# 512-column matmuls for both token halves in gate and up

## The chip, the cores and the metric

One core of a Trainium2 chip runs the whole kernel. The metric is device time in microseconds of one execution, the median of several. Engines are named as in the profile: PE (TensorE matmuls; PEld its weight loads), DVE (VectorE), ACT (ScalarE), POOL (GpSimd), SP (SyncE, which here only issues transfers). SBUF is the on-chip memory of 128 partitions, PSUM the matmuls' accumulator memory; a bank of it holds 512 fp32 columns.

## The reference

One decoder layer on 512 tokens of width 1024 in float32: a mixer (retention heads beside indexed sparse attention) with a residual LayerNorm, and then the feed-forward part, which the change is about:

```
gate, up = jnp.split(x @ w_gate_up, 2, axis=-1)        # x: 512 x 1024, w_gate_up: 1024 x 5632
ffn = (jax.nn.silu(gate) * up) @ w_down                # 2816 hidden features
return layer_norm(DEEPNORM_ALPHA * x + ffn, ln_ffn_gain, ln_ffn_bias)
```

## The kernel before

**fp32 by parts.** PE multiplies float32r operands, so each operand is split into a high part (ACT casts it) and a low part (the rest: DVE subtracts, or ACT writes minus the high part and a DMA issued by POOL adds the source onto it). A product is high x high + low x high + high x low, three matmuls for each block of 128 of the inner dimension. `split`, line 84, does this.

**Gate and up by seven products.** x and the weights are cut into 2 x 2 blocks: two halves of 256 tokens, two halves of 512 inner features, and the gate and the up column of a tile pair; the four outputs (gate and up of both token halves) come from seven products in place of eight (Strassen's scheme in Winograd's form). The stage goes over NF = 22 tiles of 128 hidden features, `order` gives their sequence, and `g_load(n)` brings a tile's gate and up weights (1 MB) into `graw[n]`, one of three buffers. The token side is made once in `parts`: "11", "12", "22" are blocks of x, "s1" to "s4" sums of them; each has a high and a low half, [partition, high or low, k, 256 tokens]. The weight side is made for each tile: B is gate's two blocks as they are, A, C and D come from the sums of `g_sum` (four DVE operations of 512 columns) and from up. `g_conv(n, kind)` splits them, two blocks of 512 columns each for A, B and C and one for D, into buffers of which each of the high and the low kind has four.

`g_mm(n, acc, kind, i, q, first)`, line 849, is one product: 12 matmuls of 256 columns, four k times (high, low) with the high tokens and high with the low tokens, into bank `acc`. A tile has banks a, b (PSUM tag "d", four banks in all) and c (tag "u", four banks). `g_cycle(n)`, line 883, issues one tile's products on PE, in this order in the steady state: A0(n) into a; A1(n) into c; B0(n+1) into a(n+1); C0(n) into a; B1(n+1) into b(n+1); C1(n) into a; D(n) into c. Between them a copy of bank a is taken three times, as the sums of the scheme need: after B0 (`g_t1`, to h1), after A0 (t2), after C0 (t7), and silu reads it at the end (h2). On DVE `g_add1` adds b to h1, t7 gets c, and `g_end(n-1)` adds c to t2 and multiplies: h1 = silu(gate) x up for one token half, h2 for the other. `hT(n)` is where h1 and h2 lie (`hu`).

The order of all engines is written out by hand (the schedule is manual: each engine takes its instructions in program order, and semaphores hold one back until its inputs are there and its buffer is free). Tiles n < FIRST = 4 go beside the end of the mixer and have special cases in `g_cycle`; 4 to 21 are the steady state. Behind the loop `prepare_down` splits the first blocks of w_down and of h, interleaved with the last tile by `next(between)`, and the down projection follows: matmuls of 512 columns for blocks m = 0 to 3 and 10 (`conv_w`, `conv_h`, `d_mm`), then a scheme of seven products for the rest.

SP issues the weight loads in program order; POOL issues the accumulating DMAs. In the steady state before, POOL has none, since all of `g_conv` there uses DVE.

Of the kernel before, what the change touches and what calls it, by code (L numbers as in the profile page):

```python
# [53 lines left out]
def hybrid_layer_kernel(ctx: ExitStack, tc: tile.TileContext, xT, x, pos, w0, wf, wt, wo,  # L54
# [761 lines left out]
    def g_sum(n, eng=V, which=slice(0, 4)):
        if n >= NF:
            return
        g, u = graw[n][:, 0], graw[n][:, 1]
        if n not in gsum:  # L820
            gsum[n] = [tmp(f"gs{n}_{i}") for i in range(4)]
        t = gsum[n]
        for dst, a, b in ((0, u[:, :S], g[:, :S]), (1, u[:, S:], t[0]), (2, u[:, S:], u[:, :S]), (3, g[:, S:], t[1]))[which]:
            eng.tensor_tensor(t[dst], a, b, op=ALU.subtract)  # L824
# [24 lines left out]
    def g_mm(n, acc, kind, i, q, first):
        h, l = gw[n, kind]  # L850
        steps = [(k, a, b) for k in range(4) for a, b in ((h, 0), (l, 0), (h, 1))]
        if n == 0:
            steps.sort(key=lambda x: x[2])
        for j, (k, a, b) in enumerate(steps):
            T.matmul(gp[n][acc], lhsT=a[:, i * S + k * P:i * S + k * P + P], rhs=parts[q][:, b, k],  # L855
                     start=first and j == 0, stop=j == 11, skip_group_check=True)

    def g_open(n):
        h = hT(n)
        gp[n] = {"a": psd(f"ga{n}")[:, :Q], "b": (psu if n < FIRST else psd)(f"gb{n}")[:, :Q], "h1": h[:, :Q], "h2": h[:, Q:]}  # L860

    def g_t1(n):
        A.copy(gp[n]["h1"], gp[n]["a"])

    def g_add1(n):
        h1 = gp[n]["h1"]
        V.tensor_tensor(h1, h1, gp[n]["b"], op=ALU.add)
# [8 lines left out]

    def g_end(n):
        g = gp[n]
        V.tensor_tensor(g["t2"], g["t2"], g["c"], op=ALU.add)
        V.tensor_tensor(g["h1"], g["h1"], g["t2"], op=ALU.mult)  # L880
        V.tensor_tensor(g["h2"], g["h2"], g["t7"], op=ALU.mult)

    def g_cycle(n, between=None):
# [10 lines left out]
        A.copy(gp[n]["t2"], gp[n]["a"])  # L894
# [16 lines left out]
        c = gp[n]["c"]  # L911
        if n == NF - 1:
            c = tmp("gc")[:, :Q]
            A.copy(c, gp[n]["c"])
            g_mm(n, "c", "D", 0, "s4", False)
        A.copy(gp[n]["t7"], gp[n]["a"])
# [8 lines left out]
        V.tensor_tensor(gp[n]["t7"], gp[n]["t7"], c, op=ALU.add)  # L925
# [60 lines left out]
    def combine(q, b, eng=V):  # L986
        if q in ("s2", "s3"):
            csum[q, b] = tmp(f"c{q}_{b}")
        src = {"s3": (kept["11", b - 2], "21"), "s2": ("22", csum.get(("s3", b))), "s1": (kept["11", b - 2], csum.get(("s2", b))),
               "s4": (kept["12", b - 2], csum.get(("s2", b)))}[q]  # L990
# [1 line left out]
        eng.tensor_tensor(csum[q, b], in0, in1, op=ALU.add if q == "s1" else ALU.subtract)
# [103 lines left out]
    def conv_w(c, k):  # L1096
        if k == 10 and c == 0:
            wprep((c, k), d10)
        else:
            t, i = (r5b, 2) if k == 10 else (draw[c, k // 2], 2 * (k % 2))  # L1100
            wprep((c, k), [t[:, i:i + 2].rearrange("p k c -> p (k c)")])

    def conv_h(m):
# [141 lines left out]
        V.scalar_tensor_tensor(y[b], in0=y[b], scalar=mv[:, 0:1], in1=gf[:, 0], op0=ALU.subtract, op1=ALU.mult)  # L1245

    def prepare_down():
        conv_w(0, 0)
        conv_h(0)
        yield  # L1250
        conv_w(0, 1)
        conv_h(1)
        yield
# [257 lines left out]
```

## Time and profile before

| what | value |
|---|---|
| median of 3 runs (lowest, highest) | 619.25 us (618.81, 619.79) |
| the profiled execution: own time, span | 619.74 us, 617.9 us |
| PE clock granted, mean | 0.996 |
| x's parts and tiles 0 to 3 (273 to 312.4 us of the span) | PE idle 0.64 us in all |
| tiles 4 to 21 (about 312 to 498 us) | PE without idle time |
| DMA share over ten of these tiles (332.6 to 433.3 us) | 0.30 |

The profile is one execution, on the hardware's profiler. A row of a timeline is start and duration in us, engine, line of the kernel, operation, tile written <- tiles read, shapes; in square brackets the idle time of the engine before it and what ended it. A row with xN holds N instructions in a row. In rows grouped by line the numbers at the end are busy time in us and the mean of one in ns, and then the idle time before them. A row of windows gives, for a stretch of the span, the busy us of each engine with its instruction count, the clock granted to PE, the mean busy share of the 16 DMA engines, and GB/s. A DMA row ends with the KB of one transfer and the median us from issue to landing. Rows of PE overlap, since the end of one matmul lies in the next; the distance of two starts is what a matmul costs in a stream.

### The profile page before, as it was taken

How to read it: one execution, taken by the hardware profiler on the slowest of the kernel's cores; microseconds unless marked ns; L12 is line 12 of the kernel's file. 1: busy time of each engine (PE TensorE's matmuls, PEld its weight loads, DVE VectorE, ACT ScalarE, POOL GpSimd, SP SyncE). 2: the span in 40 equal slices, each digit the busy share in tenths (PEclk: the TensorE clock that was granted, in tenths of full speed). 3: DMA queues.
4: the chain of work that ended last, by engine and by line, in shares of the span. 5: the costliest groups of instructions: out<-in, count | busy, mean ns of one | idle time of the engine just before them, and what ended most of it. 6: DMA issues, size and time to landing. Idle time of an engine off the chain costs nothing.

```text
span 617.9 us, 9846 instructions
## 1 busy us (share of the span) xinstructions
PE 608.2 (98%) x3732; PEld 545.6 (88%) x3732; DVE 512.8 (83%) x953; ACT 323.0 (52%) x576; POOL 114.0 (18%) x118
## 2 busy tenths in 40 slices
PE   9999999999999999999999999999999999999994
PEld 7988888888888878889999999999999988888884
DVE  6897687898879877979998989898888888977856
ACT  5643444334343765777754555555455685648300
POOL 1176232421455000242000000000000021214010
PEclk9999999999999999999999999999999999999998
DMA  9887444778533962596333232332323379589602
GB/s 307 290 227 207 132 112 126 185 177 218 136 103 102 322 266 94 134 232 131 91 132 137 74 133 85 121 100 106 118 88 124 102 192 221 157 226 300 195 35 102
DMA packets 31584, 97.97 MB, mean 159 GB/s; under 512 B 3328, under 2 KB 9024, under 8 KB 25904
## 3 DMA queue, kind: packets, MB, share of 16 engines
q1 hardware_dynamic: 20464, 76.23, 35.9%
q0 software_dynamic: 10336, 19.86, 17.9%
q10 hardware_dynamic: 736, 1.25, 0.6%
q8 instruction: 29, 0.48, 0.3%
q14 instruction: 19, 0.16, 0.1%
HBM read 74.52 MB, written 2.10 MB: 124 GB/s over the span
## 4 chain that ended last, share of the span: by engine, by line
PE 82%; DVE 6%; issue 5%; DMA 3%; POOL 2%; ACT 1%; POOLq 0%; DVEq 0%; ACTq 0%
PE ga L855 19%; PE gc L855 10%; PE pf L95 5%; PE pf L94 5%; PE pf L96 5%; PE gb L855 4%; PE acc L205 4%; PE dl L95 2%; PE dl L96 2%; PE dl L94 2%; PE pt L94 2%; PE pt L96 2%; PE pt L95 2%; PE dr L96 2%; PE dr L95 2%
## 5 line engine op out<-in xcount | busy, mean ns | idle before, releaser
L86 ACT CAST wh<-raw 128x1024 fp32r<-128x1024 f32 x43 | 45.0, 1050 | 50.9 <-issue 20.6
L89 POOL DMA_DIRECT2D slot<-hu x9 | 10.9, 1337 | 235.0 <-ACT slot L88 233.8
L94 PE MATMUL pf<-xh,wh 128*128 128x512 f32 x128 | 50.0, 391 | 0.0
L95 PE MATMUL pf<-xl,wh 128*128 128x512 f32 x128 | 50.0, 390 | 0.0
L96 PE MATMUL pf<-xh,wl 128*128 128x512 f32 x128 | 49.9, 390 | 0.0
L91 DVE TENSOR_TENSOR wl<-raw,wh 128x1024 fp32r<-128x1024 f32 x24 | 29.1, 1224 | 14.2 <-ACT wh L86 14.2
L94 PE MATMUL pt<-wh,xh 128*128 128x512 f32 x96 | 39.1, 408 | 0.0
L96 PE MATMUL pt<-wh,xl 128*128 128x512 f32 x96 | 37.6, 391 | 0.0
L95 PE MATMUL pt<-wl,xh 128*128 128x512 f32 x96 | 37.5, 390 | 0.0
L824 DVE TENSOR_TENSOR gs<-graw,gs 128x512 f32<-128x512 f32 x44 | 30.3, 689 | 0.8
L440 POOL TENSOR_TENSOR rs<-ve,half 128x1 f32<-128x1 f32 (+1 forms) x11 | 11.8, 1069 | 102.6 <-DVE ve L439 102.4
L824 DVE TENSOR_TENSOR gs<-graw 128x512 f32<-128x512 f32 x44 | 30.2, 685 | 0.0
L96 PEld LDWEIGHTS pf<-xh,wl 128*128 128x128 f32 x128 | 24.0, 188 | 5.1
L94 PEld LDWEIGHTS pf<-xh,wh 128*128 128x128 f32 x128 | 24.0, 188 | 4.6
L95 PEld LDWEIGHTS pf<-xl,wh 128*128 128x128 f32 x128 | 24.1, 188 | 4.5
L89 POOL DMA_DIRECT2D wl<-raw x19 | 16.9, 891 | 59.2 <-ACT wl L88 52.3
L402 DVE MAX8 m<-score 128x8 f32<-128x256 f32 (+2 forms) x48 | 26.8, 558 | 1.1
L403 DVE MATCH_REPLACE8 score<-m,score 128x256 f32<-128x256 f32 (+2 forms) x48 | 26.0, 543 | 0.0
L385 ACT ACTIVATE lg<-lg 128x256 f32<-128x256 f32 (+2 forms) x24 | 10.9, 474 | 24.6 <-PE lg L384 22.6
L96 PEld LDWEIGHTS pt<-wh,xl 128*128 128x128 f32 x96 | 18.0, 188 | 3.9
L95 PEld LDWEIGHTS pt<-wl,xh 128*128 128x128 f32 x96 | 18.1, 189 | 3.1
L94 PEld LDWEIGHTS pt<-wh,xh 128*128 128x128 f32 x96 | 18.1, 188 | 3.1
(1123 smaller groups left out, 2076.3 us busy)
## 6 DMA issues: line engine op xcount, KB each, us to landing
graw<-in_wgu_dram SPq DMA_DIRECT2D x22, 1024.0 KB, 4.8
wl<-raw POOLq DMA_DIRECT2D x19, 512.0 KB, 5.6
raw<-in_wf_dram SPq DMA_DIRECT2D x8, 1024.0 KB, 7.4
raw<-in_wo_dram SPq DMA_DIRECT2D x8, 1024.0 KB, 4.8
raw<-in_wt_dram SPq DMA_DIRECT2D x6, 1024.0 KB, 5.5
r<-in_wd_dram SPq DMA_DIRECT2D x12, 512.0 KB, 5.6
draw<-in_wd_dram SPq DMA_DIRECT2D x8, 512.0 KB, 5.8
w0s<-in_w_dram SPq DMA_DIRECT2D x8, 320.0 KB, 4.8
```

The source lines that it names most:

```text
L86: A.copy(hi, src)
L89: nc.gpsimd.dma_start(lo.bitcast(F32), src, accum_op=ALU.add)
L91: eng_lo.tensor_tensor(lo, src, hi.bitcast(F32), op=ALU.subtract)
L94: T.matmul(acc, lhsT=lh, rhs=rh, start=first, stop=False, **kw)
L95: T.matmul(acc, lhsT=lh, rhs=rl, start=False, stop=False, **kw)
L96: T.matmul(acc, lhsT=ll, rhs=rh, start=False, stop=last, **kw)
L205: T.matmul(acc0[i][:, o:], lhsT=a[:, i * P:i * P + P], rhs=b[kt][:, o:], start=(kt == 0 and p == 0), stop=(kt == KT - 1 and p == 2))
L402: V.max(m8, a)
L403: V.match_replace(out=a, in_to_replace=m8, in_values=a, imm_value=TAKEN)
L440: G.tensor_tensor(r[:, :n], e[:, :n], half[:, :n], op=ALU.pow)
L824: eng.tensor_tensor(t[dst], a, b, op=ALU.subtract)
L855: T.matmul(gp[n][acc], lhsT=a[:, i * S + k * P:i * S + k * P + P], rhs=parts[q][:, b, k], start=first and j == 0, stop=j == 11, skip_group ...
```

## The change

For tiles 4 to 21 (`wide(n)`) a product takes 8 matmuls instead of 12: the high weights move the high and the low token part in one matmul of 512 columns into the two halves of a full bank, and the low weights the high tokens alone, 256 columns. The two halves of each accumulator are added later by DVE (`g_join`).

```diff
 def g_mm(n, acc, kind, i, q, first):
     h, l = gw[n, kind]
+    if wide(n):
+        ws = [slice(i * S + k * P, i * S + k * P + P) for k in range(4)]
+        for k in range(4):
+            T.matmul(two(gp[n][acc]), lhsT=h[:, ws[k]], rhs=parts[q][:, :, k], start=first and k == 0, stop=False, ...)
+        for k in range(4):
+            T.matmul(gp[n][acc][:, :Q], lhsT=l[:, ws[k]], rhs=parts[q][:, 0, k], start=False, stop=k == 3, ...)
+        return
```

`g_cycle` still issues tiles 0 to 3; 4 to 20 go through the new `g_wide`, 21 through `g_last`. Two of a tile's four weight sums leave DVE: the first (gate + up) is loaded as up's block by `g_ahead` into one of four slots of a kept unit (`firsts`, in the place of "s9"), and gate's block is added by a DMA of POOL straight from memory (`g_plus1`); the third is added in place in `graw` by a DMA of POOL (`g_plus3`). The signs are turned: the four sums are additions now.

```diff
+def g_ahead(n):      # SP
+    dma(firsts(n), wgu[order[n], :, 1, :S])
+def g_plus1(n):      # POOL
+    nc.gpsimd.dma_start(firsts(n), wgu[order[n], :, 0, :S], accum_op=ALU.add)
+def g_plus3(n):      # POOL
+    u = graw[n][:, 1]
+    nc.gpsimd.dma_start(u[:, :S], u[:, S:], accum_op=ALU.add)
 def g_sum(n, eng=V, which=slice(0, 4)):
+    if n >= FIRST:
+        t = gsum[n] = [firsts(n), tmp(f"gs{n}_1"), u[:, :S], tmp(f"gs{n}_3")]
+        eng.tensor_tensor(t[1], u[:, S:], t[0], op=ALU.add)
+        eng.tensor_tensor(t[3], g[:, S:], t[1], op=ALU.add)
+        return
...
+def g_hi(n, kind):   # the casts of g_conv alone, on ACT
+def g_lo(n, kind, eng=V):   # its low parts alone: DVE, or with eng None ACT and a DMA of POOL
+def g_join(t):
+    V.tensor_tensor(t[:, :Q], t[:, :Q], t[:, Q:], op=ALU.add)
 def g_add1(n):
-    h1 = gp[n]["h1"]
-    V.tensor_tensor(h1, h1, gp[n]["b"], op=ALU.add)
+    h = gp[n]["h" if wide(n) else "h1"]
+    V.tensor_tensor(h, h, gp[n]["b"], op=ALU.add)
+    if wide(n):
+        g_join(h)
+def g_minus(n, t, acc):
+    A.activation(gp[n][t], gp[n][acc], AF.Copy, scale=-1.0)
+def g_seven(n):      # t7 = -a on ACT; the DVE part: t7 -= c
+def g_h2(n):         # DVE: h2 += a[:, :Q]
+def g_t2(n):         # DVE: t2 -= c, then g_join
+def g_mult(n):       # DVE: h1 *= t2, h2 *= t7
+def g_wide(n):
+    old = wide(n - 1)
+    g_mm(n, "a", "A", 0, "s2", False)
+    if n > FIRST:
+        g_lo(n, "C")
+    g_hi(n, "D")
+    g_lo(n, "D", None)
+    g_plus3(n + 2)
+    g_plus1(n + 4)
+    g_load(n + 3)
+    if old:
+        g_h2(n - 1)
+        g_t2(n - 1)
+    else:
+        g_end(n - 1)
+    gp[n]["t2"], gp[n]["t7"] = tmp(f"gt{n}"), tmp(f"gu{n}")
+    g_minus(n, "t2", "a")
+    if old:
+        A.activation(gp[n - 1]["h2"], gp[n - 1]["h2"], AF.Silu)
+        g_mult(n - 1)
+    gp[n]["c"] = psu(f"gc{n}")
+    g_mm(n, "c", "A", 1, "s1", True)
+    g_hi(n + 1, "A")
+    g_lo(n + 1, "A")
+    g_open(n + 1)
+    g_mm(n + 1, "a", "B", 0, "11", True)
+    g_t1(n + 1)
+    g_mm(n, "a", "C", 0, "s3", False)
+    g_seven(n)()
+    g_join(gp[n]["t7"])
+    g_mm(n + 1, "b", "B", 1, "12", True)
+    g_add1(n + 1)
+    g_hi(n + 2, "B")
+    g_lo(n + 2, "B")
+    g_silu1(n + 1)
+    g_mm(n, "a", "C", 1, "22", False)
+    g_hi(n + 1, "C")
+    A.copy(gp[n]["h2"], gp[n]["a"][:, Q:])
+    g_sum(n + 2)
+    g_mm(n, "c", "D", 0, "s4", False)
+    g_ahead(n + 5)
```

`g_last` has the products A0, A1, C0, D, C1, where D goes into a bank of its own ("gd") and is subtracted by DVE; before, ACT copied c away so that D could follow in it. `prepare_down` now yields four times, and the joins and products of tiles 20 and 21 stand on DVE behind its four splits:

```diff
+def g_last(n, between):
+    g_mm(n, "a", "A", 0, "s2", False)
+    g_lo(n, "C"); g_hi(n, "D"); g_lo(n, "D"); g_h2(n - 1); g_minus(n, "t2", "a")
+    g_mm(n, "c", "A", 1, "s1", True)
+    next(between); next(between)
+    g_mm(n, "a", "C", 0, "s3", False)
+    seven = g_seven(n)
+    g["d"] = psd("gd")
+    g_mm(n, "d", "D", 0, "s4", True)
+    next(between); next(between)
...
+    g_mm(n, "a", "C", 1, "22", False)
...
+    g_t2(n - 1); seven(); g_join(g["t7"]); g_mult(n - 1)
+    V.tensor_tensor(g["t2"], g["t2"], g["d"], op=ALU.subtract)
+    g_t2(n); g_mult(n)
```

In `g_cycle`: t2 and t7 become minus a; `g_load(n + 4)` and D's split of the next tile are left to `g_wide` from tile 3 on; behind a cycle stand now `g_plus1(n + 4)` (n > 0), `g_plus3(n + 3)` (n = 1, 2), `g_ahead(n + 5)`, and for n = 0 also `g_ahead(4)` and `g_plus1(4)`. In `combine`, three of the four sums of x (six instructions) become scalar_tensor_tensor with scalar -1, for the sign. `dheld` moves from "s9" to "s10".

More of the change, by code (lines that the diff above doesn't have):

```diff
@@ L805, in hT, with wide @@
         if i not in hu:
-            hu[i] = unit(("X0", "X1", "s8", "s2", "s10", "s9")[i], f"hu{i}")
+            hu[i] = keep["t1"] if i == 5 else unit(("X0", "X1", "s8", "s2", "s10")[i], f"hu{i}")
         return hu[i][:, f % 4]
     graw, gp = {}, {}
+    def wide(n):
+        return n >= FIRST
     def g_load(n):
@@ L814, in g_load, with firsts @@
             dma(graw[n], wgu[order[n]])
+    def firsts(n):
+        if "t1" not in keep:
+            keep["t1"] = unit("s9", "firsts")
+        return keep["t1"][:, (n + 2) % 4]
+    def g_ahead(n):
+        if FIRST <= n < NF:
+            dma(firsts(n), wgu[order[n], :, 1, :S])
+    def g_plus1(n):
+        if FIRST <= n < NF:
+            nc.gpsimd.dma_start(firsts(n), wgu[order[n], :, 0, :S], accum_op=ALU.add)
+    def g_plus3(n):
+        if FIRST <= n < NF:
+            u = graw[n][:, 1]
+            nc.gpsimd.dma_start(u[:, :S], u[:, S:], accum_op=ALU.add)
     def g_sum(n, eng=V, which=slice(0, 4)):
@@ L823, in g_sum, with g_src @@
         for dst, a, b in ((0, u[:, :S], g[:, :S]), (1, u[:, S:], t[0]), (2, u[:, S:], u[:, :S]), (3, g[:, S:], t[1]))[which]:
-            eng.tensor_tensor(t[dst], a, b, op=ALU.subtract)
+            eng.tensor_tensor(t[dst], a, b, op=ALU.add)
     def held(n):
         return n in (0, 1)
+    def g_src(n, kind):
+        g, u, t = graw[n][:, 0], graw[n][:, 1], gsum.get(n)
+        return {"A": lambda: (t[1], t[0]), "B": lambda: (g[:, :S], g[:, S:]), "C": lambda: (t[2], t[3]),
+                "D": lambda: (u[:, S:],)}[kind]()
     def g_conv(n, kind, eng=V, into=None):
@@ L831, in g_conv @@
             return
-        g, u, t = graw[n][:, 0], graw[n][:, 1], gsum.get(n)
-        src = {"A": lambda: (t[1], t[0]), "B": lambda: (g[:, :S], g[:, S:]), "C": lambda: (t[2], t[3]),
-               "D": lambda: (u[:, S:],)}[kind]()
         if kind == "D" and n == 1:
-            both = big.tile([P, 2, S], F32R, tag="s9", name="dheld")
+            both = big.tile([P, 2, S], F32R, tag="s10", name="dheld")
             h, l = both[:, 0], both[:, 1]
@@ L841, in g_conv @@
         else:
-            h = wp.tile([P, 1024], F32R, tag="wh", bufs=4, name=f"gh{n}{kind}")
-            l = wp.tile([P, 1024], F32R, tag="wl", bufs=4, name=f"gl{n}{kind}")
-        for i, sc in enumerate(src):
+            g_hi(n, kind)
+            g_lo(n, kind, eng)
+            return
+        for i, sc in enumerate(g_src(n, kind)):
             cs = slice(i * S, i * S + S)
@@ L847, in g_conv, with two @@
         gw[n, kind] = (h, l)
+    def g_hi(n, kind):
+        if n >= NF:
+            return
+        h, l = gw[n, kind] = [wp.tile([P, 1024], F32R, tag=f"w{t}", bufs=4, name=f"g{t}{n}{kind}") for t in "hl"]
+        for i, sc in enumerate(g_src(n, kind)):
+            A.copy(h[:, i * S:i * S + S], sc)
+    def g_lo(n, kind, eng=V):
+        if n >= NF:
+            return
+        h, l = gw[n, kind]
+        for i, sc in enumerate(g_src(n, kind)):
+            cs = slice(i * S, i * S + S)
+            if eng is None:
+                A.activation(l[:, cs], sc, AF.Copy, scale=-1.0)
+                nc.gpsimd.dma_start(l[:, cs].bitcast(F32), sc, accum_op=ALU.add)
+            else:
+                eng.tensor_tensor(l[:, cs], sc, h[:, cs].bitcast(F32), op=ALU.subtract)
+    def two(t):
+        return t.rearrange("p (t c) -> p t c", t=2)
     def g_mm(n, acc, kind, i, q, first):
         h, l = gw[n, kind]
+        if wide(n):
+            ws = [slice(i * S + k * P, i * S + k * P + P) for k in range(4)]
+            for k in range(4):
+                T.matmul(two(gp[n][acc]), lhsT=h[:, ws[k]], rhs=parts[q][:, :, k], start=first and k == 0, stop=False,
+                         skip_group_check=True)
+            for k in range(4):
+                T.matmul(gp[n][acc][:, :Q], lhsT=l[:, ws[k]], rhs=parts[q][:, 0, k], start=False, stop=k == 3,
+                         skip_group_check=True)
+            return
         steps = [(k, a, b) for k in range(4) for a, b in ((h, 0), (l, 0), (h, 1))]
@@ L854, in g_mm @@
         for j, (k, a, b) in enumerate(steps):
-            T.matmul(gp[n][acc], lhsT=a[:, i * S + k * P:i * S + k * P + P], rhs=parts[q][:, b, k],
+            T.matmul(gp[n][acc][:, :Q], lhsT=a[:, i * S + k * P:i * S + k * P + P], rhs=parts[q][:, b, k],
                      start=first and j == 0, stop=j == 11, skip_group_check=True)
@@ L859, in g_open @@
         h = hT(n)
[L860 removed]
+        w = S if wide(n) else Q
+        gp[n] = {"a": psd(f"ga{n}")[:, :w], "b": (psd if wide(n) else psu)(f"gb{n}")[:, :w], "h": h, "h1": h[:, :Q], "h2": h[:, Q:]}
     def g_t1(n):
[L863 removed]
+        A.copy(gp[n]["h" if wide(n) else "h1"], gp[n]["a"])
+    def g_join(t):
+        V.tensor_tensor(t[:, :Q], t[:, :Q], t[:, Q:], op=ALU.add)
     def g_add1(n):
[L866 to L867 removed]
+        h = gp[n]["h" if wide(n) else "h1"]
+        V.tensor_tensor(h, h, gp[n]["b"], op=ALU.add)
+        if wide(n):
+            g_join(h)
     def g_silu1(n):
@@ L878, in g_end @@
         g = gp[n]
-        V.tensor_tensor(g["t2"], g["t2"], g["c"], op=ALU.add)
+        V.tensor_tensor(g["t2"], g["t2"], g["c"], op=ALU.subtract)
         V.tensor_tensor(g["h1"], g["h1"], g["t2"], op=ALU.mult)
         V.tensor_tensor(g["h2"], g["h2"], g["t7"], op=ALU.mult)
+    def g_minus(n, t, acc):
+        A.activation(gp[n][t], gp[n][acc], AF.Copy, scale=-1.0)
+    def g_seven(n):
+        g = gp[n]
+        g_minus(n, "t7", "a")
+        return lambda: V.tensor_tensor(g["t7"], g["t7"], g["c"], op=ALU.subtract)
@@ new lines, in g_h2 @@
+    def g_h2(n):
+        g = gp[n]
+        V.tensor_tensor(g["h2"], g["h2"], g["a"][:, :Q], op=ALU.add)
+    def g_t2(n):
+        g = gp[n]
+        V.tensor_tensor(g["t2"], g["t2"], g["c"], op=ALU.subtract)
+        g_join(g["t2"])
+    def g_mult(n):
+        g = gp[n]
+        V.tensor_tensor(g["h1"], g["h1"], g["t2"][:, :Q], op=ALU.mult)
+        V.tensor_tensor(g["h2"], g["h2"], g["t7"][:, :Q], op=ALU.mult)
+    def g_wide(n):
[11 more added lines that the diff above has]
+            g_t2(n - 1)
+        else:
+            g_end(n - 1)
[25 more added lines that the diff above has]
+        g_ahead(n + 5)
@@ new lines, in g_last @@
+    def g_last(n, between):
+        g, o = gp[n], gp[n - 1]
+        g_mm(n, "a", "A", 0, "s2", False)
+        g["t2"], g["t7"] = tmp(f"gt{n}"), tmp(f"gu{n}")
+        g_lo(n, "C")
+        g_hi(n, "D")
+        g_lo(n, "D")
+        g_h2(n - 1)
+        g_minus(n, "t2", "a")
+        g["c"] = psu(f"gc{n}")
+        g_mm(n, "c", "A", 1, "s1", True)
+        next(between)
+        next(between)
+        g_mm(n, "a", "C", 0, "s3", False)
+        seven = g_seven(n)
+        g["d"] = psd("gd")
+        g_mm(n, "d", "D", 0, "s4", True)
+        next(between)
+        next(between)
+        A.activation(o["h2"], o["h2"], AF.Silu)
+        g_mm(n, "a", "C", 1, "22", False)
+        A.copy(g["h2"], g["a"][:, Q:])
+        g_h2(n)
+        A.activation(g["h2"], g["h2"], AF.Silu)
+        g_t2(n - 1)
+        seven()
+        g_join(g["t7"])
+        g_mult(n - 1)
+        V.tensor_tensor(g["t2"], g["t2"], g["d"], op=ALU.subtract)
+        g_t2(n)
+        g_mult(n)
@@ L893, in g_cycle @@
         gp[n]["t2"], gp[n]["t7"] = t[:, :Q], t[:, Q:]
-        A.copy(gp[n]["t2"], gp[n]["a"])
+        g_minus(n, "t2", "a")
         if n == 1:
@@ L897, in g_cycle @@
                 g_silu1(m)
-        if n not in (1, 2, 3):
+        if n == 0:
             g_conv(n + 1, "A")
@@ L910, in g_cycle @@
             g_mm(3, "b", "B", 1, "12", True)
[L911 to L916, printed above, removed]
+        less = g_seven(n)
         if n == 0:
@@ L924, in g_cycle @@
             g_sum(2, V, slice(2, 4))
-        V.tensor_tensor(gp[n]["t7"], gp[n]["t7"], c, op=ALU.add)
+        less()
         if n in (2, 3):
             g_conv(n + 1, "A")
-        if between:
-            next(between)
         if n == 2:
@@ L949, in g_cycle @@
             g_sum(2, V, slice(0, 2))
-        if n < NF - 1 and not held(n):
+        if not held(n):
             g_mm(n, "c", "D", 0, "s4", False)
         A.activation(gp[n]["h2"], gp[n]["a"], AF.Silu)
-        g_conv(n + 1, "D", V if n else None)
-        g_load(n + 4)
+        if n < FIRST - 1:
+            g_conv(n + 1, "D", V if n else None)
+            g_load(n + 4)
+        if n:
+            g_plus1(n + 4)
+        if n in (1, 2):
+            g_plus3(n + 3)
+        if n == 0:
+            g_ahead(4)
+            g_plus1(4)
+        g_ahead(n + 5)
     g_load(0)
@@ L988, in combine @@
             csum[q, b] = tmp(f"c{q}_{b}")
-        src = {"s3": (kept["11", b - 2], "21"), "s2": ("22", csum.get(("s3", b))), "s1": (kept["11", b - 2], csum.get(("s2", b))),
+        src = {"s3": (kept["11", b - 2], "21"), "s2": ("22", csum.get(("s3", b))), "s1": (csum.get(("s2", b)), kept["11", b - 2]),
                "s4": (kept["12", b - 2], csum.get(("s2", b)))}[q]
         in0, in1 = (turned[t, b] if isinstance(t, str) else t for t in src)
-        eng.tensor_tensor(csum[q, b], in0, in1, op=ALU.add if q == "s1" else ALU.subtract)
+        if q == "s3":
+            eng.tensor_tensor(csum[q, b], in0, in1, op=ALU.subtract)
+        else:
+            eng.scalar_tensor_tensor(csum[q, b], in0=in0, scalar=-1.0, in1=in1, op0=ALU.mult, op1=ALU.subtract)
     def hi(q, b):
@@ L1247, in prepare_down @@
     def prepare_down():
[L1248 to L1253, printed above, removed]
+        for m in range(2):
+            conv_w(0, m)
+            yield
+            conv_h(m)
+            yield
     for n in range(NF - 2):
-        g_cycle(n)
+        (g_wide if wide(n) else g_cycle)(n)
     d_load(0, 0)
-    g_cycle(NF - 2)
+    g_wide(NF - 2)
     d_load(0, 1)
-    g_cycle(NF - 1, prepare_down())
-    g_end(NF - 1)
+    g_last(NF - 1, prepare_down())
     def r1_load(j):
```

2 lines of the change are left out of this document (1 added, 1 removed).

## The prediction

> **What bounds the kernel now.** I read the page first (busy shares, then the chain that ended last), then the table of windows for the gate-and-up stage, then the timelines of PE, DVE and ACT there.
>
> ```profile
> PE 608.2 (98%) x3732; PEld 545.6 (88%) x3732; DVE 512.8 (83%) x953; ACT 323.0 (52%) x576; POOL 114.0 (18%) x118
> PE 82%; DVE 6%; issue 5%; DMA 3%; POOL 2%; ACT 1%; POOLq 0%; DVEq 0%; ACTq 0%
> PE ga L855 19%; PE gc L855 10%; PE pf L95 5%; PE pf L94 5%; PE pf L96 5%; PE gb L855 4%; PE acc L205 4%; PE dl L95 2%; PE dl L96 2%; PE dl L94 2%; PE pt L94 2%; PE pt L96 2%; PE pt L95 2%; PE dr L96 2%; PE dr L95 2%
> core 0: us, PE busy (x) PEld busy (x) DVE busy (x) ACT busy (x) POOL busy (x), PEclk, DMA share, GB/s
> 332.60:433.30 100.70, 100.70 (x842) 100.70 (x841) 86.38 (x161) 55.38 (x120) 0.00 (x0) 1.00 0.30 106
> ```
>
> The first three lines are of the page: 82% of the chain is PE work, a third of the span being line 855, the matmuls of gate and up. The window covers ten tiles: PE has no idle time at full granted clock, DVE is busy 8.64 us of each 10.07 us tile, ACT 5.5, POOL nothing. PE is the bound, so shorter matmuls pay until another engine fails to follow. DVE has only 1.4 us to spare, so the question is what it has to do per tile afterwards, and when.
>
> **What a wider matmul saves.** PE timeline, start and duration in us; the 512-column rows are in the feature projections, the 256-column rows in gate and up.
>
> ```profile
> 119.92 0.39 PE L94 MATMUL pf<-xh,wh 128*128 128x512 f32 x1
> ...
> 124.00 0.39 PE L94 MATMUL pt<-wh,xh 128*128 128x512 f32 x1
> ...
> 483.77 0.28 PE L855 MATMUL ga<-part,gh21B 128*128 128x256 f32 x1
> ...
> 485.21 0.28 PE L855 MATMUL ga<-parts,gh20C 128*128 128x256 f32 x1
> ...
> 486.53 0.28 PE L855 MATMUL ga<-parts,gh20C 128*128 128x256 f32 x1
> ```
>
> Eighteen 512-column starts lie between 119.92 and 124.00: 0.2267 us each. Twelve 256-column starts lie between 483.77 and 485.21: 0.120 each. The difference, 106.7 ns, is what 256 columns cost, so 13.3 ns go with each matmul whatever its width. One of the seven products of a tile is now 12 x 0.120 = 1.44 us; it becomes 4 x 0.2267 + 4 x 0.120 = 1.387 us. Seven products: 10.08 before (the window agrees), 9.71 after. Tiles 4 to 21 have 126 products, so PE sheds 126 x 0.053 = 6.7 us (504 matmuls fewer). The new moving operand is two blocks of 256 from two places of a tile; no row shows one. Its ends are 0.2267 and two separate 256s, 0.240; I take 0.2267, since both are the same count of columns in one instruction.
>
> The Trainium skill, page "TensorE: Matmul & The Clock Gate", section "Wait — 56ns, not 53.3ns?", speaks against that size: it puts the fixed part of a warm matmul at about 2.5 ns, so the same 504 matmuls would be worth an estimated 1.3 us. The trace disagrees, with 13.3 ns per matmul, and I go by the trace; the page's case is under the rivals.
>
> **What the wider sums cost DVE.** Each accumulator now holds two halves that must be added. A tile's DVE list, from g_wide, in its order: low parts of C (2 of 512 columns); h2 (256); t2 minus c (512, PSUM), join (256); two products (256); low parts of A (2); t7 minus c (512, PSUM), join; h1 plus b (512, PSUM), join; low parts of B (2); two sums (512). Off DVE go the low part of D and one sum (now accumulating DMAs of GpSimd) and another sum (a plain load plus such a DMA). Prices from the DVE timeline of one tile:
>
> ```profile
> 388.18 1.29 DVE L91 TENSOR_TENSOR gl12B<-graw,gh12B 128x512 fp32r<-128x512 f32 x2 [1.31 <-ACT gh12B L86]
> 389.39 0.42 DVE L867 TENSOR_TENSOR hu<-hu,gb 128x256 f32<-128x256 f32 x1
> 389.72 0.69 DVE L824 TENSOR_TENSOR gs<-graw 128x512 f32<-128x512 f32 x1
> 390.44 0.69 DVE L824 TENSOR_TENSOR gs<-graw,gs 128x512 f32<-128x512 f32 x1
> 391.05 0.68 DVE L824 TENSOR_TENSOR gs<-graw 128x512 f32<-128x512 f32 x1
> ...
> 394.06 0.42 DVE L879 TENSOR_TENSOR gt<-gt,gc 128x256 f32<-128x256 f32 x1
> 394.51 0.42 DVE L880 TENSOR_TENSOR hu<-hu,gt 128x256 f32<-128x256 f32 x1
> 394.86 0.42 DVE L881 TENSOR_TENSOR hu<-hu,gt 128x256 f32<-128x256 f32 x1
> 575.11 0.69 DVE L1226 TENSOR_TENSOR x<-x,dl 128x512 f32<-128x512 f32 x1
> 575.83 0.69 DVE L1229 BATCH_NORM_STATS2 fst<-x 128x6 f32<-128x512 f32 x1
> ```
>
> Start to start: a pair of 512s 1.21; a 256 before independent work 0.33 (from PSUM, too); a 512 whose result the next one reads 0.72, else 0.61; a 256 read by the next 0.45. A 512 from PSUM read by the next is 0.72 as well (575.11 to 575.83). The list: 3 x 1.21 + 0.33 + (0.72 + 0.45) + 0.35 + 0.33 + 2 x (0.72 + 0.33) + 0.72 + 0.61 = 9.2 us. That is under 9.71, so DVE's total does not bind. Its order may.
>
> **The chain that closes on itself.** PSUM has four banks for a and b together, so a(n+2) takes the bank of a(n), and product B0(n+2), which stands third in the next tile's cycle, waits until DVE has read a(n) in g_h2(n). In g_wide that read stands behind t7, h1+b, B's lows, the sums and C's lows. The hand-overs:
>
> ```profile
> 486.85 0.37 ACT L916 COPY gt<-ga 128x256 f32<-128x256 f32 x1 [1.07 <-PE ga L855]
> 487.25 0.42 DVE L925 TENSOR_TENSOR gt<-gt,gc 128x256 f32<-128x256 f32 x1
> L692 ACT COPY kept<-tr 128x512 f32<-128x512 f32 x4 | 2.3, 586 | 0.7 <-PE tr L674 0.7
> 273.80 1.28 DVE L971 SCALAR_TENSOR_TENSOR x<-z,rs,gbm 128x1024 f32<-128x1024 f32 x1 [0.68 <-POOL rs L440]
> 275.23 1.07 PE L674 MATMUL tr<-ident,x 128*128 128x128 f32 x8 [0.23 <-DVE x L971]
> 387.53 1.14 ACT L86 CAST gh12B<-graw 128x512 fp32r<-128x512 f32 x2 [1.11 <-PE gb L855]
> ```
>
> ACT reads a PSUM bank 0.32 us after its last matmul started (486.53, 486.85); DVE follows ACT after 0.03 (487.22, 487.25); a 512-column copy out of PSUM is 0.59; PE follows DVE after 0.15 (275.08, 275.23). From the start of B0(n+1): the last matmul of C0(n) starts at 2 x 1.387 - 0.12 = 2.65; ACT's t7 copy 2.97 to 3.56; DVE at 3.59; t7 4.31, join 4.64, h1+b 5.36 (B1 is ready at 4.36), join 5.69, B's lows 6.90, sums 7.62 and 8.23, C's lows 9.44, h2 ends 9.86, PE starts B0(n+2) at 10.01. ACT keeps up: two casts take 1.14 (387.53), B's are done at 5.5, silu h1 starts at 5.8, C's casts end near 7.3, the copy of h2 near 7.6. So the new period is 10.01 us, not 9.71, against 10.08 before: PE waits 0.30 at B0 in every tile. Of this sum the release of PE is the weakest term: 0.15 is the one row with DVE as releaser, 0.03 is what ACT and DVE need among themselves (period 9.89).
>
> B0(5) to B0(21) are 16 such periods: 16 x 0.30 = 4.8 us of stall. Sum: -6.7 + 4.8 = -1.9 us. The profiled execution took 619.74 us (span 617.9), 0.49 above the median of 619.25; it would become 617.8, the median 617.3.
>
> **DMA, SP and GpSimd.**
>
> ```profile
> q1 hardware_dynamic: 20464, 76.23, 35.9%
> q0 software_dynamic: 10336, 19.86, 17.9%
> graw<-in_wgu_dram SPq DMA_DIRECT2D x22, 1024.0 KB, 4.8
> slot<-hu POOLq DMA_DIRECT2D x9, 256.0 KB, 6.9
> gl0D<-graw POOLq DMA_DIRECT2D x1, 256.0 KB, 6.6
> dheld<-graw POOLq DMA_DIRECT2D x1, 256.0 KB, 3.3
> ```
>
> Over the span, 35.9% is 222 us for 76.23 MB: 3.05 us of all engines per 1 MB load, 0.76 per 256 KB. The accumulating queue's 17.9% is 111 us for 19.86 MB: 1.46 us per 256 KB. A tile used 3.05 us; it will use 3.05 + 0.76 + 3 x 1.46 = 8.2 of 10.0. It fits, with little left. On POOL three issues stand in a row: D's low, plus3(n+2), which waits for the load of n+2, and plus1(n+4); the next D low is behind both. Counted from the start of B0(n+1), the low part of D(n+1) is issued at 8.6 and PE wants it at 15.6: 6.9 us of room against landings of 3.3 to 6.9. g_load moves from the end of a cycle (n+4) to near its start (n+3), and now waits for D's low to land; g_ahead(n+5) is queued behind it on SP. Landing at about 6 into the cycle, plus 4.8 (up to 8 beside the accumulations), the load is there before B's cast wants it, 17 us into it. I cost all this at nothing, hidden by PE.
>
> **The ends and small edits.**
>
> ```profile
> L992 DVE TENSOR_TENSOR kept<-kept,cs 128x512 f32<-128x512 f32 x4 | 2.7, 687 | 0.0
> L1424 DVE SCALAR_TENSOR_TENSOR x<-x,rs,gbf 128x512 f32<-128x512 f32 x6 | 4.2, 750 | 1.3 <-POOL rs L440 1.3
> 296.35 0.88 POOL L89 DMA_DIRECT2D dheld<-graw  x1 [11.20 <-ACT gt L894]
> 312.45 0.69 DVE L824 TENSOR_TENSOR gs<-graw 128x512 f32<-128x512 f32 x1
> 492.75 1.22 DVE L91 TENSOR_TENSOR dl(0, 0)_5420<-draw,dh(0, 0)_5419 128x1024 fp32r<-128x1024 f32 x1
> 501.24 1.23 DVE L91 TENSOR_TENSOR dl(0, 2)_5508<-draw,dh(0, 2)_5507 128x1024 fp32r<-128x1024 f32 x1 [0.91 <-ACT dh(0, 2)_5507 L86]
> ```
>
> The signs change add for subtract (free) and six combines to scalar_tensor_tensor: 0 to 6 x 0.063 = 0.4 us; I take 0. At the start, g_ahead(4) stands behind g_load(4), which waits for dheld (296.35 + 3.3), so with 4.8 and one accumulation of 3.3 to 6.9 tile 4's sum is ready between 308 and 312; DVE wants it near 312.4: free, at worst 1 us of DVE, whose backlog shrinks by two sums in each of cycles 2 and 3. In g_last, DVE needs 1.21 + 0.61 + 0.33 + 2 x 1.22 = 4.6 us before the first down matmul, which comes after five products, 6.9 us; the second pair is ready near 8.2 and wanted near 8.3: 0 to 0.3, I take 0. D in its own bank takes an ACT copy of c away (0.37 as 486.85) and adds a 512 subtraction to DVE (0.72) behind the last product; PE waited for neither, so it is worth nothing. The joins and products of the last two tiles (about 5 us of DVE) now stand before the lows of down's blocks 2 and 3; 501.24 had 0.91 to spare, and PE wants block 2 only 48 down matmuls (10.9 us) into down, some 1.6 after it is ready.
>
> **Rivals.**
> - The chain is shorter than 9.71 (0.30 less, by a faster release and shorter dependent steps). PE stays the bound: 619.25 - 6.7 = 612.5. For it: DVE's list is 9.2. Against: every link is a row.
> - The other side: the chain is longer. From a period of 10.13 on (16 x 0.05 eats the 0.75 us that the products outside the 16 periods save) the kernel is slower. If each of the nine DVE steps in the chain pays one more hand-over of 0.03, the period is 10.28: 16 x 0.57 - 6.7 = +2.4, 621.7. Against: the quoted starts contain such hand-overs already.
> - D's low lands late. It has 6.9 us; at 7.5 the period is 10.6 and the time 619.25 - 6.7 + 16 x 0.89 = 626.8. For it: 82% DMA use. Against: its turn comes when the engines should be nearly idle, as for dheld (3.3).
> - The width saves little. With 0.240 per 512 the product stays 1.44, PE needs 10.08, the chain is 0.11 longer at 10.12: 619.9. With a fixed part of 2.5 ns instead of 13.3 a product saves 10 ns, the chain is 10.10: 619.4; this is what the Trainium skill's page named above would give.
>
> **How the numbers follow.** Forecast 0.55 (own range 615.4 to 618.9: periods 9.89 to 10.11), PE-bound 0.15, longer chain 0.13, late D 0.09, no saving 0.08. Predicted time 617.3. The range 613.0 to 621.5 leaves out late D, half of the PE-bound case and the far end of the longer chain, 0.19 in all. No change is within 0.2%, 1.2 us. Faster: 0.15 + three quarters of 0.55 = 0.56; same: 0.14 + 0.08 + 0.02 = 0.24; slower: 0.20.
>
> **What would show it.** Product starts 1.39 apart on PE; in each tile an idle of some 0.3 us on ga (B0) released by DVE's h2 read; tile period 10.0; DVE's longest wait per tile before t7, released by ACT; POOL busy in gate and up; DMA share near 0.8 there. Wrong if PE has no idle there (then nearer 612.5), if its idle stands at gc's D product or is released by a DMA, or if 512-column starts are 0.24 apart.

## The result, and the profile after

The changed kernel took 615.01 us (median of 4 runs, 614.88 to 616.23) against 619.28 (4 runs, 618.81 to 619.79): ratio 0.9935, 95% interval 0.9918 to 0.9952. It is faster, by 0.65%, and 2.3 us below the 617.3 forecast. The profiled execution took 614.91 us, its span is 613.1.

The page of the changed kernel: busy times, and the chain that ended last.

```profile
PE 603.2 (98%) x3228; PEld 518.2 (85%) x3228; DVE 523.3 (85%) x973; ACT 350.1 (57%) x610; POOL 160.0 (26%) x171
PE 89%; DVE 5%; issue 3%; ACT 1%; POOL 1%; DMA 1%; POOLq 0%; DVEq 0%
```

504 matmuls fewer, and 5.0 us less of PE busy time. The table of windows, over about ten tile pairs (a tile pair is one tile of the stage, its gate and its up columns):

```profile
core 0: us, PE busy (x) PEld busy (x) DVE busy (x) ACT busy (x) POOL busy (x), PEclk, DMA share, GB/s
332.60:430.00 97.40, 97.40 (x557) 85.10 (x556) 90.70 (x170) 70.77 (x139) 25.78 (x30) 1.00 0.87 217
```

PE still has no idle time there; DVE went from 86% to 93%, POOL from nothing to 26%, the DMA share from 0.30 to 0.87. Next the PE timeline of the changed kernel (start, duration):

```profile
312.30 0.40 PE L905 MATMUL ga<-part,gh4B 128*128 128x512 f32 x1
...
389.57 1.09 PE L905 MATMUL gc<-parts,gh11A 128*128 128x512 f32 x4
390.50 0.63 PE L908 MATMUL gc<-parts,gl11A 128*128 128x256 f32 x4
390.97 1.09 PE L905 MATMUL ga<-part,gh12B 128*128 128x512 f32 x4
...
400.80 1.09 PE L905 MATMUL ga<-part,gh13B 128*128 128x512 f32 x4
...
493.42 0.40 PE L94 MATMUL dl<-dh(0, 0)_5040,h 128*128 128x512 f32 x1
```

and the same two ends in the kernel before:

```profile
312.41 0.28 PE L855 MATMUL ga<-part,gh4B 128*128 128x256 f32 x1
...
498.17 0.40 PE L94 MATMUL dl<-dh(0, 0)_5419,h 128*128 128x512 f32 x1
```

From the first product of tile 4 to the first down matmul: 185.76 us before, 181.12 after, 4.64 less; the spans differ by 4.8. So all but 0.2 us lies in gate and up. A tile pair takes 400.80 - 390.97 = 9.83 us, forecast 10.01, and B0(12) starts 1.40 us after A1 with no gap: no stall at B0. But four 512-column matmuls last 0.93 us from the first to what follows (389.57 to 390.50), 0.2325 each on average, not 0.2267; with 0.47 for the four of 256 a product is 1.403 us, not 1.387. 126 x (1.44 - 1.403) = 4.7 us, which is the gain of this stage.

DVE's timeline beside it:

```profile
384.79 0.69 DVE L955 TENSOR_TENSOR gu<-gu,gc 128x512 f32<-128x512 f32 x1 [0.50 <-ACT gu L950]
...
390.65 0.41 DVE L959 TENSOR_TENSOR hu<-hu,ga 128x256 f32<-128x256 f32 x1
...
394.61 0.69 DVE L955 TENSOR_TENSOR gu<-gu,gc 128x512 f32<-128x512 f32 x1 [0.49 <-ACT gu L950]
```

From t7's subtraction (384.79) to the end of the h2 read (391.06) is 6.27 us, the prediction's own sum (3.59 to 9.86). Yet PE starts B0(12) at 390.97, 0.09 us before DVE has done with a(10), so the two are not in the same bank. It is so in all 16 periods of the trace; in e4 below, where they share a bank, B0 starts only behind that end. The profile does not print bank numbers. Two questions follow: is the assumed bank the reason that the chain does not close, and why are 512-column matmuls slower here than in the feature projections?

### The profile page after: what moved, and what is told of

It is laid out like the page before. It is cut to its first block, busy times and chain, and to the rows that moved or that the text cites. A ratio compares the mean times of both kernels' runs of the same rounds, so it can differ in the third digit from the quotient of the medians.

```text
span 613.1 us, 9090 instructions
## 1 busy us (share of the span) xinstructions
PE 603.2 (98%) x3228; PEld 518.2 (85%) x3228; DVE 523.3 (85%) x973; ACT 350.1 (57%) x610; POOL 160.0 (26%) x171
## 4 chain that ended last, share of the span: by engine, by line
PE 89%; DVE 5%; issue 3%; ACT 1%; POOL 1%; DMA 1%; POOLq 0%; DVEq 0%
PE ga L905 11%; PE ga L908 6%; PE gc L905 5%; PE pf L95 5%; PE pf L94 5%; PE pf L96 5%; PE acc L205 4%; PE gb L905 3%; PE gc L908 3%; PE ga L915 3%; PE mx L96 2%; PE mx L94 2%; PE mx L95 2%; PE dl L94 2%; PE dl L95 2%
## 5 line engine op out<-in xcount | busy, mean ns | idle before, releaser
L830 POOL DMA_DIRECT2D firsts<-in_wgu_dram x18 | 19.2, 1084 | 20.3 <-DMA firsts<-in_wgu_dram 18.2
L835 POOL DMA_DIRECT2D graw<-graw x18 | 17.9, 992 | 10.4 <-DVE hu L968 3.6
```

Source lines behind the costliest of these rows:

```text
L830: nc.gpsimd.dma_start(firsts(n), wgu[order[n], :, 0, :S], accum_op=ALU.add)
```

## The experiments

Eleven kernels; the ratio is to the kernel before on the same chip.

| label | us | ratio, 95% interval |
|---|---|---|
| e1_narrow | 619.78 | 1.0002 (0.9991 to 1.0012) |
| e2_oneblock | 614.82 | 0.9917 (0.9903 to 0.9932) |
| e3_alternate | 616.62 | 0.9942 (0.9929 to 0.9956) |
| e4_ownbanks | 618.65 | 0.9982 (0.9974 to 0.9991) |
| e5_dlow_dve | 615.88 | 0.9931 (0.9918 to 0.9944) |
| e6_sums_dve | 624.32 | 1.0072 (1.0058 to 1.0086) |
| e7_d_in_c | 618.48 | 0.9982 (0.9973 to 0.9991) |
| e8_all512 | 667.43 | one run |
| e9_paired | 614.32 | 0.9911 (0.9897 to 0.9924) |
| e10_three | 614.25 | 0.9913 (0.9899 to 0.9927) |
| e11_again | 615.11 | 0.9923 (0.9910 to 0.9935) |

**e1_narrow: is all of it the width?**

```diff
-T.matmul(two(gp[n][acc]), lhsT=h[:, ws[k]], rhs=parts[q][:, :, k], ...)
+for t in range(2):
+    T.matmul(gp[n][acc][:, t * Q:t * Q + Q], lhsT=h[:, ws[k]], rhs=parts[q][:, t, k], ...)
```

> The changed kernel with every 512-column matmul of gate and up issued as two 256-column matmuls into the two halves of the same bank; the new order of ACT, DVE and GpSimd, the rings and the own bank of D stay. If the whole gain is TensorE time of the wider form, a product goes from 1.403 us back to 12 x 0.120 = 1.44, seven of them 10.08 in place of 9.82 per tile, and 126 x 0.037 = 4.7 us come back: about 619.6, within 0.2% of the kernel before. If the new order carries a part of the gain by itself (a wait at the boundary that it removes), the time stays below 618.5.

619.78 us, the kernel before to 0.02%. In its PE timeline B0 of two tile pairs stands 10.08 apart, a product 1.44 again:

```profile
392.27 1.12 PE L906 MATMUL ga<-part,gh12B 128*128 128x256 f32 x8
...
402.35 1.12 PE L906 MATMUL ga<-part,gh13B 128*128 128x256 f32 x8
```

From its first product of tile 4 (311.63) to its first down matmul (497.39) it takes 185.76 us, as the kernel before does to the hundredth. With narrow matmuls the new order is worth nothing; the width is worth everything.

**e4_ownbanks: is the bank the point?** Tiles of even and of odd number get banks of their own (the last D takes one of b's).

```diff
+def bank(which, n):
+    if (which, n % 2) not in fixed:
+        fixed[which, n % 2] = psd(f"g{which}p{n % 2}")
+    return fixed[which, n % 2]
 def g_open(n):
+    if wide(n):
+        gp[n] = {"a": bank("a", n), "b": bank("b", n), ...}
```

> The changed kernel with the banks of a and b fixed: a(n+2) takes the bank of a(n), b(n+2) that of b(n), where the changed kernel's trace has a(n+3) in the bank of a(n). If the chain of the prediction was right but for the bank, it closes now: B0(n+2) waits for g_h2(n), the period is 2 x 1.403 + 3.6 less the overlap + 6.27, about 10.04 against 9.82, TensorE idles some 0.2 us at B0 of each tile pair with DVE as the releaser, and 16 x 0.22 = 3.5 us are added: about 618.5. If the bank was never the point (some slack hides it), the time is 615.0 within 0.4.

618.65 us, as expected. PE's timeline, then DVE's, then a row of the waits between 332.6 and 430 us (us in total, times, longest):

```profile
382.15 1.21 PE L905 MATMUL gap<-part,gh11B 128*128 128x512 f32 x4
...
390.68 1.09 PE L905 MATMUL gc<-parts,gh11A 128*128 128x512 f32 x4
391.61 0.63 PE L908 MATMUL gc<-parts,gl11A 128*128 128x256 f32 x4
392.23 1.20 PE L905 MATMUL gap<-part,gh12B 128*128 128x512 f32 x4
...
402.30 1.18 PE L905 MATMUL gap<-part,gh13B 128*128 128x512 f32 x4
```

```profile
385.90 0.69 DVE L965 TENSOR_TENSOR gu<-gu,gc 128x512 f32<-128x512 f32 x1 [0.74 <-ACT gu L960]
...
391.76 0.41 DVE L969 TENSOR_TENSOR hu<-hu,gap 128x256 f32<-128x256 f32 x1
```

```profile
PEld gap L905 <- DVE hu L969: 1.7, 9, 0.2
```

B0 now starts 0.06 us after the h2 read ends (391.76 + 0.41), 0.15 later than 390.68 + 1.40 would allow, and its four matmuls last 1.20 instead of 1.09. The wait is entered at PE's weight load for B0, and what ends it is DVE's h2 read, in each of the nine periods of that window. The period is 10.07 us: the stall that the prediction described, at the place and of about the size that it gave (10.01, or 10.04 with the product of 1.403). Two terms are off against each other: PE follows DVE after 0.06, not 0.15, and t7 stands 3.75 us behind B0 (382.15 to 385.90), not 3.59, since the products are longer and B0 starts slowly after its wait. The stall was absent from the changed kernel only because there a(n+2) does not take a(n)'s bank. Which bank it takes there is open: no view shows the a(n+3) of the expectation above.

**e2, e3, e8, e9: why 0.2325?** e2 makes the moving operand one block, e3 alternates the widths, e8 has no 256s, e9 puts them first in three products of a pair.

```diff
 # e2
-parts[q] = big.tile([P, 2, 4, 2 * P], F32R, ...)
+parts[q] = big.tile([P, 4, 2, 2 * P], F32R, ...)
 # e3: one loop over k in place of two
-for k in range(4):
 # e8
-T.matmul(gp[n][acc][:, :Q], lhsT=l[:, ws[k]], rhs=parts[q][:, 0, k], ...)
+T.matmul(two(gp[n][acc]), lhsT=l[:, ws[k]], rhs=parts[q][:, :, k], ...)
 # e9
+order = [(k, b) for b in ((0, 1) if first or kind == "D" else (1, 0)) for k in range(4)]
```

> The changed kernel with the operand `parts` laid out so that the 512 columns of a matmul are one contiguous block (high or low parts of both token halves side by side) and not two blocks of 256. If the 0.233 us between 512-column matmuls (0.227 for the down products) comes of the moving operand's two blocks, a product becomes 4 x 0.2267 + 4 x 0.120 = 1.387 us and the kernel is 126 x 0.016 = 2.0 us faster than the changed one: about 613.0. If it comes of what stands next to them (the 256-column matmuls, the weights), nothing moves: 615.0 within 0.4.

> The changed kernel with the order of a product's eight matmuls changed: 512, 256, 512, 256 and so on, in place of four and four; weights and operands the same. If the 0.006 us above the 0.227 belongs to a 512-column matmul itself, nothing moves (615.0 within 0.4). If it belongs to neighbours (a weight load that the shorter matmul before it covers less well), each of the four 512s now follows a 256 and the product changes by some 0.02 us, 126 times: 2 to 3 us to one side or the other.

> The changed kernel with the four 256-column matmuls of a product (low weights by high activations) widened to 512 columns, which adds the product of the two low parts. A product then is eight 512-column matmuls and nothing else. If the 0.2325 us between 512-column matmuls comes of having 256-column ones beside them, the distance falls to the 0.2267 of the down products: 1.813 us per product and 615.0 + 126 x 0.410 = about 667. If the operands of gate and up make it, it stays at 0.2325: 1.860 us and about 673.

> The changed kernel with the 256-column matmuls ahead of the 512-column ones in the products A0, C0 and C1, so that four changes from 256 to 512 columns are left in a tile pair in place of seven. If such a change costs the 0.016 us by which a product is above 1.387, three of them fewer in 18 tile pairs give 18 x 3 x 0.016 = 0.9 us: about 614.1, and a period of 9.77 in place of 9.82. If the cost sits in each 512-column matmul of a mixed stream, the period stays at 9.82 and the time at 615.0 within 0.4.

PE timelines of e2, of e3, of e8 and of e9:

```profile
391.37 1.09 PE L905 MATMUL ga<-part,gh12B 128*128 128x512 f32 x4
...
401.19 1.09 PE L905 MATMUL ga<-part,gh13B 128*128 128x512 f32 x4
```

```profile
389.82 0.40 PE L905 MATMUL gc<-parts,gh11A 128*128 128x512 f32 x1
...
391.23 0.40 PE L905 MATMUL ga<-part,gh12B 128*128 128x512 f32 x1
```

```profile
384.35 1.07 PE L905 MATMUL ga<-parts,gh9A 128*128 128x512 f32 x4
...
398.85 1.07 PE L905 MATMUL gc<-parts,gh10A 128*128 128x512 f32 x4
```

```profile
384.67 1.09 PE L910 MATMUL ga<-part,gh10C 128*128 128x512 f32 x4
385.60 1.07 PE L910 MATMUL gc<-parts,gh10D 128*128 128x512 f32 x4
386.51 0.64 PE L907 MATMUL gc<-parts,gl10D 128*128 128x256 f32 x4
...
389.77 1.09 PE L910 MATMUL ga<-part,gh12B 128*128 128x512 f32 x4
...
399.55 1.09 PE L910 MATMUL ga<-part,gh13B 128*128 128x512 f32 x4
```

e2: period 9.82, and 181.12 us from tile 4 (312.70) to down (493.82), as in the changed kernel; the two blocks are not the cause. e3: a product of 1.41 us in place of 1.403. Its time is 1.5 us above e11's, a little less than the 2 to 3 expected; the intervals overlap, so it is the trace that shows a change (182.40 us from tile 4 to down, 1.28 more than in the changed kernel). e8: the 64 matmuls from 384.35 to 398.85 stand 0.2266 us apart, and the time is the 667 of the first theory: the same operands at the same place run at full pace when all matmuls are wide (one run). e9: in a run of eight wide matmuls the first four take 0.93 us, the next four 0.91 (0.2275 each), and the period falls to 9.78 us, as expected. Both groups of four stand beside the same work of DVE and DMA, so that work does not explain the difference. So a 512-column matmul takes some 6 ns more, on average, while it stands among the first four after a 256-column one. Net of slightly shorter 256s (0.47 in place of 0.48) that is 0.016 us per product in the changed kernel, 2.0 us over 126. What in TensorE makes it is open; no run here looks further.

**e5_dlow_dve and e6_sums_dve: how near is DVE?** e5 gives it the low part of D back, e6 the two sums.

```diff
 # e5
-g_lo(n, "D", None)
+g_lo(n, "D")
 # e6 (g_ahead, g_plus1 and g_plus3 do nothing)
+for dst, a, b in ((0, u[:, :S], g[:, :S]), (1, u[:, S:], t[0]), (2, u[:, S:], u[:, :S]), (3, g[:, S:], t[1])):
+    eng.tensor_tensor(t[dst], a, b, op=ALU.add)
```

> The changed kernel with the low part of D by DVE again, in place of a copy by ACT and an accumulating DMA. DVE's list per tile pair grows by one subtraction of 128x512, from 9.1 us of work and 0.5 of waits to about 9.7 of work, against a period of 9.82 that TensorE sets. If DVE still fits beside TensorE, the time stays at 615.0 within 1. If its waits cannot shrink, the period becomes 9.7 + 0.5 = 10.2 and 16 x 0.4 = 6 us are added: about 621.

> The changed kernel without the ring of sums prepared by GpSimd: the two sums per tile pair that come out of that ring are DVE's again (D's low part stays with the DMA). DVE's list grows by two additions of 128x512, 1.3 us, to about 10.4 us of work against TensorE's 9.82. If DVE is so near to being the bound, the period becomes 10.4 to 10.9 and 16 x 0.6 to 1.1 = 10 to 17 us are added: 625 to 632, with TensorE waiting for DVE at B0 or at A0. If DVE has more room than its busy time tells, the time stays under 618.

DVE's timeline in e5, then in e6, each row one tile pair after the other:

```profile
384.74 0.68 DVE L955 TENSOR_TENSOR gu<-gu,gc 128x512 f32<-128x512 f32 x1
...
394.57 0.68 DVE L955 TENSOR_TENSOR gu<-gu,gc 128x512 f32<-128x512 f32 x1
```

```profile
389.05 0.68 DVE L955 TENSOR_TENSOR gu<-gu,gc 128x512 f32<-128x512 f32 x1
...
399.49 0.68 DVE L955 TENSOR_TENSOR gu<-gu,gc 128x512 f32<-128x512 f32 x1
```

e5: 9.83 us, and the wait before t7 (0.50 in the changed kernel) is gone; the time is 615.88, its ratio within the interval of the changed kernel's. DVE's list, one subtraction longer, now has no gap left: it is about 9.83 - 0.60 = 9.23 us in the changed kernel, where the prediction summed 9.2. From tile 4 (312.14) to down (493.26) PE takes 181.12 us, as in the changed kernel, so D's DMA buys nothing. e6: 10.44 us with no wait in DVE's rows; DVE is the bound. The time is 624.32, just below the 625 to 632 expected: DVE has no waits to add, which is the low end of the expectation (period 10.4, and 16 x 0.6 is 9.6, put there as 10). PE waits for it through ACT. This is a row of e6's waits (us in total, times, longest), then one of ACT's timeline, whose silu waits for DVE's h2 before the copies that PE needs:

```profile
PE ga L905 <- ACT gu L950: 5.4, 15, 0.4
```

```profile
396.55 0.42 ACT L989 ACTIVATE hu<-hu 128x256 f32<-128x256 f32 x1 [2.01 <-DVE hu L959]
```

The ring of sums is worth 9 us to the changed kernel: without it the wider matmuls lose.

**e7_d_in_c: the own bank of D at the end.**

```diff
-seven = g_seven(n)
-g["d"] = psd("gd")
-g_mm(n, "d", "D", 0, "s4", True)
+g_seven(n)()
 next(between); next(between)
 ...
+g_mm(n, "c", "D", 0, "s4", False)
 g_mm(n, "a", "C", 1, "22", False)
 ...
-seven()
-V.tensor_tensor(g["t2"], g["t2"], g["d"], op=ALU.subtract)
```

> The changed kernel without the own bank of D in the last tile pair: C1 comes ahead of D, and D accumulates into c again, once DVE has read c for t7. If the own bank hides a wait, TensorE stands still ahead of D until DVE's subtraction is done, 0.3 to 0.8 us by the room between C0's end and C1's end (1.4 us) against ACT's copy and DVE's subtraction (0.6 + 0.7 and their releases): 615.3 to 615.8. If there was nothing to hide, 615.0 within 0.3 and no such wait in the trace.

The text above is wrong in one thing: in the kernel that ran, D is still ahead of C1. It took 618.48 us, 3.4 more than e11, far above what was expected. PE's row and DVE's rows:

```profile
492.97 1.20 PE L905 MATMUL gc<-parts,gh21D 128*128 128x512 f32 x4 [1.81 <-DVE gu L955]
```

```profile
489.96 1.22 DVE L91 TENSOR_TENSOR dl(0, 0)_5041<-draw,dh(0, 0)_5040 128x1024 fp32r<-128x1024 f32 x1 [0.96 <-ACT dh(0, 0)_5040 L86]
491.10 1.22 DVE L91 TENSOR_TENSOR h<-hu,h 128x1024 fp32r<-128x1024 f32 x1
492.24 0.68 DVE L955 TENSOR_TENSOR gu<-gu,gc 128x512 f32<-128x512 f32 x1
```

PE waits 1.81 us for a subtraction that stands on DVE behind two splits for the down projection, one of its weights and one of h (1.22 each), which the expectation had left out. The profiled executions of e7 and of the changed kernel are 3.0 us apart: 2.1 from tile 4 (312.68) to the first down matmul (495.87), which hold this wait, 0.4 ahead of tile 4 and 0.5 in down. e10, whose down part is that of the changed kernel, is 0.6 us longer there in its profiled execution, so the 0.5 need not come of the edit; its cause stays open. With the splits behind it or with ACT copying c away, as before the change, D in c may cost less; that was not run.

**e10_three and e11_again.** e10 takes over e9's order and puts the wide matmuls of A1 and B0 together, with the narrow ones of both behind them. e11 is the changed kernel again.

```diff
+g_mm(n, "c", "A", 1, "s1", True, 0)
+g_mm(n + 1, "a", "B", 0, "11", True, 0)
+g_mm(n, "c", "A", 1, "s1", True, 1)
+g_mm(n + 1, "a", "B", 0, "11", True, 1)
```

> The paired order carried one step further: the 512-column matmuls of A1 and of B0 stand together, and then the 256-column ones of both, so that three changes from 256 to 512 columns are left in a tile pair in place of four (seven in the changed kernel). If each change costs 0.016 us, the period falls from 9.78 to 9.76 and the time by 0.3 us against the paired order, 1.2 us against the changed kernel: about 613.8. If a longer run of 512-column matmuls buys nothing more, or if c and a finish too late for ACT and DVE (A1 ends 0.93 us later), the period stays at 9.78 or rises with waits of TensorE at C0 or C1.

> The changed kernel itself, unaltered, on the same chip as the two others of this set, so that they are compared with it and not only with the kernel before: 615.0 within 0.5, a ratio to the kernel before of 0.992 to 0.995.

e10's PE timeline:

```profile
389.52 1.07 PE L912 MATMUL ga<-part,gh12B 128*128 128x512 f32 x4
...
399.29 1.07 PE L912 MATMUL ga<-part,gh13B 128*128 128x512 f32 x4
```

Period 9.77, between the two expectations; 614.25 us, no different from e9. e11 took 615.11 us, as expected. Against e11 (615.11) e9 and e10 are 0.8 us lower, and their intervals overlap e11's, so the time alone does not settle it. The trace does for e9: from its first product of tile 4 to its first down matmul

```profile
311.46 1.09 PE L910 MATMUL ga<-part,gh4B 128*128 128x512 f32 x4
...
491.71 0.39 PE L94 MATMUL dl<-dh(0, 0)_5040,h 128*128 128x512 f32 x1
```

are 180.25 us, 0.87 less than in the changed kernel (0.9 expected). The same stretch of e10 (311.72 to 491.86) is 180.14, a further 0.11 in place of the 0.3 expected. e9 and e10 are the best versions found, and their times do not tell them apart.

## Why the prediction was right in sign, and where its steps failed

**PE as the bound: right.** PE has no idle time in tiles 4 to 21, before or after; with the same order but narrow matmuls (e1) the gain is nil.

**The width: right mechanism, mis-sized term.** 6.7 us predicted, 4.7 measured. The 0.2267 came from a stream of wide matmuls alone, and e8 shows that it holds for such a stream; four wide ones behind four narrow ones take 0.2325. The prediction did bound this price, with 0.240 as the far end, but for another reason, the two blocks, which cost nothing (e2). By the Trainium skill's page "TensorE: Matmul & The Clock Gate", section "Wait — 56ns, not 53.3ns?", the fixed part is about 2.5 ns per matmul, an estimated 1.3 us for 504 of them; the measured 4.7 us are 9 ns for each, so the trace still disagrees with that rule.

**DVE's list: right.** 9.2 us summed, 9.23 by e5. That its order can bind where its sum does not is what e4 shows; without the ring of sums the sum itself binds (e6).

**The closing chain: the step that failed.** Its links on DVE were right: 6.27 us from t7 to the end of the h2 read, to the hundredth. The sentence "so a(n+2) takes the bank of a(n)" was not. It was inferred from four banks for two accumulators, taking the banks to go round in turn; the trace of the changed kernel has B0(12) written while a(10) is read. With that sentence made true (e4) the period is 10.07 and 3.6 us of the 4.3 us gain are lost. By the prediction's own sign ("Wrong if PE has no idle there") its mechanism failed: it gave 0.55 to periods from 9.89 to 10.11 and 0.15 to PE as the bound, and the period was 9.82. That the time is only 2.3 us off, inside the stated range, is in part luck, since two errors had opposite signs. The predicted stall of 4.8 us became nothing and the width fell short by 2.0: with both put right the sum is -4.7, 614.6 from the median of before. The profiled executions differ by 4.8; the medians by 4.3, mostly because the profiled run of before lay 0.5 above its median.

**DMA, SP and GpSimd at nothing: right.** The accumulating DMAs are there, and the share of 0.87 in place of the predicted 0.82. The page's issues (KB each, us to landing):

```profile
graw<-in_wgu_dram SPq DMA_DIRECT2D x22, 1024.0 KB, 6.9
firsts<-in_wgu_dram SPq DMA_DIRECT2D x18, 256.0 KB, 7.1
firsts<-in_wgu_dram POOLq DMA_DIRECT2D x18, 256.0 KB, 6.5
graw<-graw POOLq DMA_DIRECT2D x18, 256.0 KB, 4.0
```

The big load takes 6.9 in place of 4.8 us, as the 4.8 to 8 given for it. None of it is waited for by PE, whose waits in the whole span are these (us in total, times, longest):

```profile
PE warm L188 <- DVE cold L185: 1.2, 1, 1.2
PE acc L205 <- ACT xh L196: 0.4, 1, 0.4
PE ga L915 <- ACT gt L950: 0.2, 1, 0.2
PE as L552 <- DVE mrl L451: 0.2, 1, 0.2
PE rz L528 <- POOL rzz L521: 0.2, 1, 0.2
```

e5 takes one of the three accumulations per tile pair away and moves nothing.

**The ends at nothing: right as a sum.** The stretches outside gate and up account for 0.2 us. But "worth nothing" for D's own bank holds only against the kernel before: inside the new order, with D left ahead of C1, the bank hides a wait of 1.8 us (e7).

**The rivals.** "PE stays the bound" is what happened, by another way than its shorter links, and at 615.0 instead of its 612.5, of which 2.0 are the 0.2325. "The width saves little" was right in part: 4.7 of 6.7 us are left, not nothing. The longer chain did not occur. D's low landed in 3.2 to 5.0 us, inside its 6.9 of room, so it was not late.

## What to carry to other kernels

A chain that closes through a buffer is only as good as the knowledge of which buffer is reused: read it off (a write that starts while the supposed previous owner is still read refutes it in one line) before a stall is put into the sum. Take the price of an instruction from a row with the same neighbours, not only the same shape. And when a bound engine is relieved, count what the next one has left: here DVE has 0.6 us of 9.8, and the preparation moved to DMA is what makes the gain possible at all.
